# A hybrid encoder layer on one core: the recurrent chain's steps move off VectorE

## The chip, the cores and the metric

The kernel runs on one core of a Trainium2 chip. The time is the device time of one execution in microseconds. Of the engines, PE multiplies matrices, DVE and POOL work elementwise on vectors, ACT copies and evaluates functions, and SP starts most of the transfers. Each engine works through its own list of instructions in order.

## The reference

One layer over 1024 tokens of width 1024. A projection feeds two branches. The first is attention with a forgetting bias. The second is a recurrence with a state of 64x64 in each of 8 heads:

```python
def frame_step(state, inp):
    r_t, w_t, k_t, v_t, kk_t, a_t = inp
    sa = jnp.einsum('bhij,bhj->bhi', state, -kk_t)
    state = (state * w_t[:, :, None, :] + sa[..., None] * (kk_t * a_t)[:, :, None, :]
             + v_t[..., None] * k_t[:, :, None, :])
    return state, jnp.einsum('bhij,bhj->bhi', state, r_t)
```

The branches are gated, summed, projected and normalised. Then every token looks up experts: scores against keys, a top-k of 16 for each of 8 heads, and for each chosen expert a row of a table u and a row of a table v:

```python
h = jax.nn.gelu(jnp.einsum('thkd,td->thk', u_table[idx], xb), approximate=False)
return jnp.einsum('thk,thkd->td', gate * h, v_table[idx])
```

A second normalisation ends the layer.

## The kernel before

The tokens go in two halves of 512. For each half the kernel does the attention (`fox`), the recurrence (`rwkv_half`) and the merge with the first normalisation and the keys' scores (`merge_half`, `queries`). Behind both halves comes the dense stage (`dense_block`), which does three tiles of 128 tokens against all experts; the other five tiles are done with gathered rows.

The recurrence is done in chunks of 64 tokens, 8 chunks in a half, two heads (e = 0, 1) at a time. That makes four units in a half (`unit(ct)`). In a unit, PE makes the products of all chunks (tile pm, L915 to L916), and DVE masks them into M (L918): the first 64 columns with "not after", the last 64, called LT, with "before". Then a triangular system is inverted in six levels m = 0 to 5. In each, PE multiplies LT with Tm, DVE masks the product to the blocks of that level (x, L942), PE multiplies x with Vm, and DVE adds the results to Tm and Vm (L947, L952, L958). After the levels come W_, At (L993), Q (L999) and the eight steps of the state sigma, whose copies go to DVE and ACT by turns (L1010). `wait` lets in other work on PE between the steps: the projections of the next unit (`elem`), which end on DVE and ACT, and of the gates.

The order on PE is that of the code. On DVE, ACT and POOL a scheduler sets it when the kernel is built. Beside all this runs background work from the second half on, of two kinds: top-k of the scores on DVE (`topk`, from L1290), and expert rows gathered by POOL (L1389) into five buffers g, each multiplied with the token and summed on DVE (L1394, an instruction on 128x1024 and a short one that reads the sum). It is let in by `mm`: each matmul adds its reckoned time to a credit, and background steps are taken from the list while there is credit:

```python
us = max(n, 256) / 2400.0 if r.dtype == F32R else max(4 * n, 256) / 2400.0
g.V.tick(us)
if not g.V.busy:
    g.B.tick(us)
```

POOL also makes most of the low parts of the split weights (L295, wl) and a few steps of `elem` (L863, L864, L868, L883).

Of the kernel before, what the change touches and what calls it, by code (L numbers as in the profile page):

```python
# [83 lines left out]
def _tables():  # L84
# [11 lines left out]
    for m in (1, 2, 4, 8, 16, 32):  # L96
        lev.append(((s[:, None] // m) % 2 == 1) & (c64[None] // m == s[:, None] // m - 1))
# [624 lines left out]
def rwkv_half(g, hf, X, kt):  # L722
# [12 lines left out]
    with ExitStack() as fx:  # L735
# [164 lines left out]
        def unit(ct):  # L900
# [3 lines left out]
            def wait(us):  # L904
                F.fill(WAIT * us)

            items = [(e, c) for c in range(NC) for e in range(2)]
            M = cp.tile([128, 2, NC, 128], F32, name="M", bufs=1)
            BK = cp.tile([128, 2, NC, 64], F32, name="BK", bufs=1)
            AV = cp.tile([128, 3, NC, 64], F32, name="AV", bufs=1)  # L910
            for u in range(0, NC, 4):
# [5 lines left out]
                for e in range(2):  # L917
                    dve.tensor_mul(M[:, e, us, :], pm[:, e], tb("m1")[:, None, :].to_broadcast([128, 4, 128]))  # L918
# [11 lines left out]
            def LT(e, c):  # L930
                return M[rows[e], e, c, 64:128]

# [3 lines left out]
            Tm, Vm = None, None  # L936
            for m in range(6):
                px = psS.tile([128, NC, 64], F32, name="s")
                for e, c in items:
                    mm(g, px[rows[e], c, :], LT(e, c), i64[rows[e]] if Tm is None else Tm[rows[e], c, :], True, True)  # L940
                x = cp.tile([128, NC, 64], F32, name="x")
                dve.tensor_mul(x, px, lev[:, m:m + 1, :].to_broadcast([128, NC, 64]))  # L942
                wait(WT[2])
                if m < 5:
                    Tn = cp.tile([128, NC, 64], F32, name="Tm")
                    if Tm is None:
                        dve.tensor_add(Tn, x, i64b)  # L947
                    else:
                        pt = psS.tile([128, NC, 64], F32, name="s")
                        for e, c in items:  # L950
                            mm(g, pt[rows[e], c, :], Vm[rows[e], c, :], x[rows[e], c, :], True, True)
                        dve.tensor_add(Tn, pt, Tm)  # L952
                    Tm = Tn
                pv = psS.tile([128, NC, 64], F32, name="s")
                for e, c in items:
                    mm(g, pv[rows[e], c, :], x[rows[e], c, :], i64[rows[e]] if Vm is None else Vm[rows[e], c, :], True, True)
                Vn = cp.tile([128, NC, 64], F32, name="V")
                dve.tensor_add(Vn, pv, i64b if Vm is None else Vm)  # L958
                Vm = Vn
                wait(WT[3])  # L960
                if m == 1:

                    px = psS.tile([128, NC, 64], F32, name="s")
                    for e, c in items:
                        o = rows[1 - e]
                        mm(g, px[rows[e], c, :], M[o, e, c, 64:128], AV[o, e, c, :], True, True)
                    act.copy(AV[:, 2], px)
            wait(WT[4])
            W_ = cp.tile([128, NC, 64], F32, name="x")
# [13 lines left out]
            pa = psS.tile([128, NC, 64], F32, name="s")  # L983
            for e, c in items:
                r = rows[e]
                mm(g, pa[r, c, :], W_[r, c, :], BK[r, e, c, :], True, True)
            At = cp.tile([128, NC, 64], F32, name="Tm")
            if SM & 16:
                pool.tensor_mul(At, i64b, E.dgc[:, :, None].to_broadcast([128, NC, 64]))
                dve.tensor_add(At, At, pa)  # L990
# [3 lines left out]
            pq = psS.tile([128, NC, 64], F32, name="s")  # L994
            for e, c in items:
                r = rows[e]
                mm(g, pq[r, c, :], W_[r, c, :], M[r, e, c, 0:64], True, True)
            Q = cp.tile([128, NC, 64], F32, name="x")
            dve.tensor_add(Q, pq, arv[:, :, 0, :])  # L999
# [848 lines left out]
```

## Time and profile before

| | us |
|---|---|
| median of 3 runs | 3691.41 (3689.55 to 3696.35) |
| the profiled execution | 3689.26 |
| its span, first to last instruction | 3687.5 |
| PE busy in the span | 3232.5 (88%) |
| DVE busy | 2366.5 (64%) |
| POOL busy | 2243.2 (61%) |
| ACT busy | 1241.6 (34%) |

The shares are averages over stages of different kinds. The recurrence of the first half lies at about 180 to 480 us, that of the second half at about 1140 to 1555 us (four units of 103 to 105 us), the merge and the scores of the second half up to about 1870 us, and the dense stage from there on. A row of waits says which engine stood idle until which instruction of another had ended.

### The profile page before, as it was taken

To read this page: it belongs to the slowest core of one execution; us is meant where nothing else is said; L and a number is where in the kernel's file an instruction comes from. 1 tells how busy PE (TensorE), PEld (TensorE's weight loads), DVE (VectorE), ACT (ScalarE), POOL (GpSimd) and SP (SyncE) were. 2 spreads that over 40 slices of the span, in tenths; PEclk is the share of its full clock that TensorE was granted. 3 is DMA by queue.
4 is the path that set the end of the run, shared out by engine and by line. 5 is a ranking of instruction groups with operands and counts; after the bars stand their busy time and mean duration, and the time that the engine had idled before them with its cause. 6 is when DMAs were issued, how large, how long until landed. Compare 5 with 4: busy or idle time off the path is not lost. (4 is left out here: it accounts for less than half of the span.)

```text
span 3687.5 us, 55563 instructions
## 1 busy us (share of the span) xinstructions
PE 3232.5 (88%) x20656; PEld 2334.0 (63%) x20656; DVE 2366.5 (64%) x5125; ACT 1241.6 (34%) x2530; POOL 2243.2 (61%) x1752
## 2 busy tenths in 40 slices
PE   7899998989987877667868867899998999999998
PEld 5577777875565656546733322587776777777666
DVE  3235423558889998899669955477665767675324
ACT  3443222333443221222234433333333333333333
POOL 2031115326566556677846566688887888886773
PEclk9999999998888777889989989899999999999999
DMA  4121124548877777877869999899999999999994
GB/s 144 52 92 45 45 96 137 189 140 283 262 262 263 243 233 247 295 259 258 309 245 397 395 343 371 337 364 361 385 383 331 392 398 396 394 396 355 403 394 164
DMA packets 338127, 1019.61 MB, mean 277 GB/s; under 512 B 46272, under 2 KB 84928, under 8 KB 336064
## 3 DMA queue, kind: packets, MB, share of 16 engines
q0 software_dynamic: 184320, 671.17, 49.0%
q1 hardware_dynamic: 141424, 324.11, 24.7%
q10 hardware_dynamic: 12112, 20.78, 1.5%
q8 instruction: 162, 2.65, 0.3%
q14 instruction: 109, 0.89, 0.1%
HBM read 960.81 MB, written 55.12 MB: 276 GB/s over the span
## 5 line engine op out<-in xcount | busy, mean ns | idle before, releaser
L1389 POOL DMA_INDIRECT g<-u,eidx x640 | 789.0, 1233 | 397.1 <-DVE hh L1394 114.5
L1394 DVE CUSTOM_DVE_ANT_0 g<-g,ext 128x1024 f32<-128x1024 f32 x640 | 862.5, 1356 | 165.2 <-DMA g<-u,eidx 164.1
L295 POOL TENSOR_TENSOR wl<-wraw,wh 128x1024 fp32r<-128x1024 f32 x131 | 323.7, 2471 | 503.4 <-ACT wh L294 475.6
L1689 POOL DMA_INDIRECT vr<-v,ve x428 | 458.6, 1072 | 193.0 <-issue 99.9
L277 PE MATMUL pg<-vr,win 128*32 128x512 f32 x1712 | 322.4, 633 | 81.9 <-DMA vr<-v,ve 81.1
L277 PE MATMUL b<-xh,uh 128*128 128x384 f32 x1024 | 352.3, 344 | 22.1 <-DVE C L1574 22.0
L277 PE MATMUL b<-xh,ul 128*128 128x384 f32 x1024 | 348.9, 341 | 1.3 <-POOL ul L295 1.1
L277 PE MATMUL b<-xl,uh 128*128 128x384 f32 x1024 | 348.8, 341 | 0.0
L294 ACT CAST wh<-wraw 128x1024 fp32r<-128x1024 f32 x150 | 157.2, 1048 | 505.1 <-PE pj L277 280.2
L277 PE MATMUL v<-vl,ch 128*128 128x512 f32 x768 | 305.9, 398 | 11.2 <-POOL vl L295 11.1
L277 PE MATMUL pj<-xh,wh 128*128 128x512 f32 x624 | 289.9, 465 | 21.1 <-ACT xh L294 7.9
L277 PE MATMUL v<-vh,ch 128*128 128x512 f32 x768 | 303.3, 395 | 0.0
L277 PE MATMUL v<-vh,cl 128*128 128x512 f32 x768 | 301.4, 392 | 0.0
L1689 POOL DMA_INDIRECT C<-v,ve x212 | 225.6, 1064 | 84.8 <-issue 54.4
L294 ACT CAST uh<-uraw 128x512 fp32r<-128x512 f32 x256 | 158.2, 620 | 350.2 <-PE b L277 322.3
L277 PE MATMUL pj<-xh,wl 128*128 128x512 f32 x624 | 262.2, 420 | 4.3 <-POOL wl L295 2.5
L277 PE MATMUL pj<-xl,wh 128*128 128x512 f32 x624 | 263.1, 422 | 2.2 <-DVE xl L295 2.2
L294 ACT CAST vh<-vraw 128x512 fp32r<-128x512 f32 x256 | 157.7, 620 | 217.7 <-PE v L277 182.9
L277 PEld LDWEIGHTS b<-xh,uh 128*128 128x128 f32 x1024 | 194.1, 190 | 55.7 <-DVE C L1574 26.0
L295 POOL TENSOR_TENSOR ul<-uraw,uh 128x512 fp32r<-128x512 f32 x128 | 168.4, 1316 | 88.3 <-ACT uh L294 86.5
L295 DVE TENSOR_TENSOR vl<-vraw,vh 128x512 fp32r<-128x512 f32 x128 | 130.0, 1016 | 143.0 <-ACT vh L294 136.0
L277 PEld LDWEIGHTS b<-xl,uh 128*128 128x128 f32 x1024 | 194.2, 190 | 14.4 <-issue 10.1
(353 smaller groups left out, 6577.5 us busy)
## 6 DMA issues: line engine op xcount, KB each, us to landing
wraw<-w SPq DMA_DIRECT2D x150, 512.0 KB, 3.4
uraw<-ut SPq DMA_DIRECT2D x128, 512.0 KB, 6.6
vraw<-vt SPq DMA_DIRECT2D x128, 512.0 KB, 7.7
cd<-S SPq DMA_DIRECT2D x12, 1344.0 KB, 10.1
C<-cd SPq DMA_DIRECT2D x63, 256.0 KB, 9.2
g<-u,eidx POOLq DMA_INDIRECT x640
gtd<-tmp ACTq DMA_DIRECT2D x32, 256.0 KB, 4.3
g<-gtd SPq DMA_DIRECT2D x32, 256.0 KB, 3.7
```

Source lines behind the costliest of these rows:

```text
L277: g.pe.matmul(o, l, r, start=start, stop=stop_)
L294: g.act.copy(hi, src)
L295: (lo_eng or g.dve).tensor_sub(lo, src, hi.bitcast(F32))
L1389: pool.indirect_dma_start(out=gg, out_offset=None, in_=A["u"], in_offset=bass.IndirectOffsetOnAxis(ap=idx[:, s_:s_ + 1], axis=0))
L1394: dve.tensor_tensor_reduce(out=gg, in0=gg, in1=xt, scale=1.0, scalar=0.0, op0=OP.mult, op1=OP.add, accum_out=hh[:, k:k + 1])
L1689: g.pool.indirect_dma_start(out=place, out_offset=None, in_=g.A["v"], in_offset=bass.IndirectOffsetOnAxis(ap=self.meta[i][1][:, t:t + 1], ...
```

## The change

The tables of the levels' masks are turned, so that a mask is laid on LT itself and not on the product. ACT copies LT out of PSUM; POOL multiplies it with the mask of each level into L (three buffers), and adds L of level 0 and the identity into Vm. PE then multiplies with the masked L, and ACT copies the product to x. AK is the part of M that was used across the heads; M keeps the first 64 columns. This holds in both halves. In the second half (hf = 1) the sums go by PE as well: a multiplication of the old value with the identity is put into the same PSUM tile first, the products are added to it, and ACT copies the result. There M and AK are copied unmasked by ACT and masked in place by POOL, the diagonal of At is laid by POOL (dg), and all copies of sigma are ACT's. In the first half the sums stay on DVE. Behind `unit` the lines of the changed kernel are 51 higher than before.

```diff
@@ -94,7 +94,8 @@
     parts["m1"] = np.concatenate([s[:, None] <= c64[None], s[:, None] < c64[None]], 1)
     lev = []
     for m in (1, 2, 4, 8, 16, 32):
-        lev.append(((s[:, None] // m) % 2 == 1) & (c64[None] // m == s[:, None] // m - 1))
+
+        lev.append(((c64[None] // m) % 2 == 1) & (s[:, None] // m == c64[None] // m - 1))
     parts["lev"] = np.concatenate(lev, 1)
     parts["i64"] = s[:, None] == c64[None]
     rst = np.ones((128, 512))
@@ -905,9 +906,13 @@
                 F.fill(WAIT * us)
 
             items = [(e, c) for c in range(NC) for e in range(2)]
-            M = cp.tile([128, 2, NC, 128], F32, name="M", bufs=1)
+            M = cp.tile([128, 2, NC, 64], F32, name="M", bufs=1)
             BK = cp.tile([128, 2, NC, 64], F32, name="BK", bufs=1)
             AV = cp.tile([128, 3, NC, 64], F32, name="AV", bufs=1)
+
+            LT = cp.tile([128, NC, 64], F32, name="LT", bufs=1)
+            AK = cp.tile([128, NC, 64], F32, name="AK", bufs=1)
+            m1 = tb("m1").rearrange("p (a t) -> p a t", a=2)
             for u in range(0, NC, 4):
                 us = slice(u, u + 4)
                 pm = psM.tile([128, 2, 4, 128], F32, name="pm")
@@ -915,7 +920,17 @@
                     for e in range(2):
                         mm(g, pm[:, e, c, :], fl(bk[rows[e], u + c, e:e + 2, :]), fl(arv[rows[e], u + c, 0:2, :]), True, True)
                 for e in range(2):
-                    dve.tensor_mul(M[:, e, us, :], pm[:, e], tb("m1")[:, None, :].to_broadcast([128, 4, 128]))
+                    act.copy(LT[rows[e], us, :], pm[rows[e], e, :, 64:128])
+                for e in range(2):
+                    o = rows[1 - e]
+                    if hf:
+                        act.copy(AK[o, us, :], pm[o, e, :, 64:128])
+                    else:
+                        dve.tensor_mul(AK[o, us, :], pm[o, e, :, 64:128], m1[o, 1:2, :].to_broadcast([64, 4, 64]))
+                if hf:
+                    act.copy(M[:, :, us, :], pm[:, :, :, 0:64])
+                else:
+                    dve.tensor_mul(M[:, :, us, :], pm[:, :, :, 0:64], m1[:, 0:1, None, :].to_broadcast([128, 2, 4, 64]))
                 wait(WT[0])
                 pt = psM.tile([128, 2, 8, 64], F32, name="pm")
                 for c in range(4):
@@ -927,46 +942,76 @@
                 act.copy(AV[:, 0:2, us, :], pt[:, :, 4:8, :])
                 wait(WT[1])
 
-            def LT(e, c):
-                return M[rows[e], e, c, 64:128]
 
             lev = tb("lev").rearrange("p (m t) -> p m t", m=6)
             i64 = tb("i64")
             i64b = i64[:, None, :].to_broadcast([128, NC, 64])
-            Tm, Vm = None, None
+            L = []
             for m in range(6):
+                L.append(cp.tile([128, NC, 64], F32, name="L", bufs=3))
+                pool.tensor_mul(L[m], LT, lev[:, m:m + 1, :].to_broadcast([128, NC, 64]))
+                if m == 0:
+
+                    Vm = cp.tile([128, NC, 64], F32, name="V", bufs=1)
+                    pool.tensor_add(Vm, L[0], i64b)
+                if hf and m == 1:
+                    pool.tensor_mul(AK, AK, m1[:, 1:2, :].to_broadcast([128, NC, 64]))
+            if hf:
+                dg = cp.tile([128, NC, 64], F32, name="L", bufs=3)
+                pool.tensor_mul(dg, i64b, E.dgc[:, :, None].to_broadcast([128, NC, 64]))
+                for e in range(2):
+                    pool.tensor_mul(M[:, e], M[:, e], m1[:, 0:1, :].to_broadcast([128, NC, 64]))
+            def grown(t=None):
+
+                pt = psS.tile([128, NC, 64], F32, name="s")
+                if hf:
+                    mm(g, pt, ident, i64b if t is None else t, True, False)
+                return pt
+
+            def summed(pt, t=None):
+
+                o = cp.tile([128, NC, 64], F32, name="Tm", bufs=1) if t is None else t
+                if hf:
+                    act.copy(o, pt)
+                else:
+                    dve.tensor_add(o, pt, i64b if t is None else t)
+                return o
+
+            def last(c):
+                return not hf or c == NC - 1
+
+            pt = grown()
+            for e, c in items:
+                mm(g, pt[rows[e], c, :], L[0][rows[e], c, :], i64[rows[e]], not hf, last(c))
+            Tm = summed(pt)
+            wait(WT[3])
+            for m in range(1, 6):
                 px = psS.tile([128, NC, 64], F32, name="s")
                 for e, c in items:
-                    mm(g, px[rows[e], c, :], LT(e, c), i64[rows[e]] if Tm is None else Tm[rows[e], c, :], True, True)
-                x = cp.tile([128, NC, 64], F32, name="x")
-                dve.tensor_mul(x, px, lev[:, m:m + 1, :].to_broadcast([128, NC, 64]))
+                    mm(g, px[rows[e], c, :], L[m][rows[e], c, :], Tm[rows[e], c, :], True, True)
+                x = cp.tile([128, NC, 64], F32, name="x", bufs=1)
+                act.copy(x, px)
+                if m < 5:
+                    pt = grown(Tm)
                 wait(WT[2])
                 if m < 5:
-                    Tn = cp.tile([128, NC, 64], F32, name="Tm")
-                    if Tm is None:
-                        dve.tensor_add(Tn, x, i64b)
-                    else:
-                        pt = psS.tile([128, NC, 64], F32, name="s")
-                        for e, c in items:
-                            mm(g, pt[rows[e], c, :], Vm[rows[e], c, :], x[rows[e], c, :], True, True)
-                        dve.tensor_add(Tn, pt, Tm)
-                    Tm = Tn
-                pv = psS.tile([128, NC, 64], F32, name="s")
+                    for e, c in items:
+                        mm(g, pt[rows[e], c, :], Vm[rows[e], c, :], x[rows[e], c, :], not hf, last(c))
+                    summed(pt, Tm)
+                pv = grown(Vm)
                 for e, c in items:
-                    mm(g, pv[rows[e], c, :], x[rows[e], c, :], i64[rows[e]] if Vm is None else Vm[rows[e], c, :], True, True)
-                Vn = cp.tile([128, NC, 64], F32, name="V")
-                dve.tensor_add(Vn, pv, i64b if Vm is None else Vm)
-                Vm = Vn
+                    mm(g, pv[rows[e], c, :], x[rows[e], c, :], Vm[rows[e], c, :], not hf, last(c))
+                summed(pv, Vm)
                 wait(WT[3])
                 if m == 1:
 
                     px = psS.tile([128, NC, 64], F32, name="s")
                     for e, c in items:
                         o = rows[1 - e]
-                        mm(g, px[rows[e], c, :], M[o, e, c, 64:128], AV[o, e, c, :], True, True)
+                        mm(g, px[rows[e], c, :], AK[o, c, :], AV[o, e, c, :], True, True)
                     act.copy(AV[:, 2], px)
             wait(WT[4])
-            W_ = cp.tile([128, NC, 64], F32, name="x")
+            W_ = cp.tile([128, NC, 64], F32, name="x", bufs=1)
             for u in range(0, NC, 8):
                 n8 = min(8, NC - u)
                 us = slice(u, u + n8)
@@ -981,22 +1026,28 @@
                     (dve.tensor_copy if e and not SM & 32 else act.copy)(AV[r, e, us, :], pw[r, :, 64:128])
             wait(WT[5])
             pa = psS.tile([128, NC, 64], F32, name="s")
+            At = cp.tile([128, NC, 64], F32, name="Tm", bufs=1)
+            if hf:
+                mm(g, pa, ident, dg, True, False)
             for e, c in items:
                 r = rows[e]
-                mm(g, pa[r, c, :], W_[r, c, :], BK[r, e, c, :], True, True)
-            At = cp.tile([128, NC, 64], F32, name="Tm")
-            if SM & 16:
-                pool.tensor_mul(At, i64b, E.dgc[:, :, None].to_broadcast([128, NC, 64]))
-                dve.tensor_add(At, At, pa)
+                mm(g, pa[r, c, :], W_[r, c, :], BK[r, e, c, :], not hf, last(c))
+            if hf:
+                act.copy(At, pa)
             else:
                 for c in range(NC):
                     dve.scalar_tensor_tensor(At[:, c, :], i64, E.dgc[:, c:c + 1], pa[:, c, :], op0=OP.mult, op1=OP.add)
             pq = psS.tile([128, NC, 64], F32, name="s")
+            if hf:
+                mm(g, pq, ident, arv[:, :, 0, :], True, False)
             for e, c in items:
                 r = rows[e]
-                mm(g, pq[r, c, :], W_[r, c, :], M[r, e, c, 0:64], True, True)
-            Q = cp.tile([128, NC, 64], F32, name="x")
-            dve.tensor_add(Q, pq, arv[:, :, 0, :])
+                mm(g, pq[r, c, :], W_[r, c, :], M[r, e, c, :], not hf, last(c))
+            Q = cp.tile([128, NC, 64], F32, name="x", bufs=1)
+            if hf:
+                act.copy(Q, pq)
+            else:
+                dve.tensor_add(Q, pq, arv[:, :, 0, :])
             wait(WT[6])
             py = psS.tile([128, NC, 64], F32, name="s")
             for c in range(NC):
@@ -1007,9 +1058,9 @@
                     mm(g, pss[r, :], BK[:, e, c, :], AV[:, e, c, :], True, False)
                 for r in rows:
                     mm(g, pss[r, :], At[r, c, :], g.sigma[r, ct, par, :], False, True)
-                (act.copy if c % 2 or SM & 64 else dve.tensor_copy)(g.sigma[:, ct, 1 - par, :], pss)
+                (act.copy if c % 2 or hf else dve.tensor_copy)(g.sigma[:, ct, 1 - par, :], pss)
                 for e, r in enumerate(rows):
-                    mm(g, py[r, c, :], AV[:, e, c, :], M[:, e, c, 0:64], True, False)
+                    mm(g, py[r, c, :], AV[:, e, c, :], M[:, e, c, :], True, False)
                 for r in rows:
                     mm(g, py[r, c, :], g.sigma[r, ct, par, :], Q[r, c, :], False, True)
                 wait(WT[7])
```

On DVE in the third unit of the second half, just behind the projection of r, before (x, Tm and V are the chain's, s and ij the top-k's, g and hh the dot products'):

```order
L942 TENSOR_TENSOR x<-s,tab 128x512
L1351 TENSOR_TENSOR s<-s 128x4x128
L947 TENSOR_TENSOR Tm<-x,tab 128x512
L1351 TENSOR_TENSOR s<-s 128x4x64
L1394 ISA g,hh<-g,ext 128x1024
L1394 ISA hh 128x1
L1351 TENSOR_TENSOR s<-s 128x4x32
L958 TENSOR_TENSOR V<-s,tab 128x512
```

and in the same place now:

```order
L758 SCALAR_TENSOR_TENSOR rt<-prev,vec,tmp 128x1
L1343 MATCH_REPLACE tmp<-tv,s 128x128
L1348 MAX_INDEX ti<-tv,s 128x8
L1445 ISA g,hh<-g,ext 128x1024
L1445 ISA hh 128x1
L1345 MAX tv<-tmp 128x8
L1341 MAX tv<-s 128x8
```

The chain's steps are gone, and top-k and dot products stand close together.

On POOL at the end of the third unit and in the fourth, before (wl is a weight's low part, g a gather of 128 rows):

```order
L295 TENSOR_TENSOR wl<-wraw,wh 128x1024
L1389 DMA g<-u,eidx 128x1024 x15
L295 TENSOR_TENSOR wl<-wraw,wh 128x1024
L1389 DMA g<-u,eidx 128x1024 x2
L295 TENSOR_TENSOR wl<-wraw,wh 128x1024
L1389 DMA g<-u,eidx 128x1024 x23
```

and now (L and V are the chain's, M and AK the copies that are masked in place):

```order
L296 TENSOR_TENSOR wl<-wraw,wh 128x1024
L952 TENSOR_TENSOR L<-LT,tab 128x512 x2
L956 TENSOR_TENSOR V<-L,tab 128x512
L958 TENSOR_TENSOR AK<-AK,tab 128x512
L952 TENSOR_TENSOR L<-LT,tab 128x512
L963 TENSOR_TENSOR M<-M,tab 128x512 x2
L952 TENSOR_TENSOR L<-LT,tab 128x512
L1440 DMA g<-u,eidx 128x1024 x2
L952 TENSOR_TENSOR L<-LT,tab 128x512
L1440 DMA g<-u,eidx 128x1024 x4
L952 TENSOR_TENSOR L<-LT,tab 128x512
L1440 DMA g<-u,eidx 128x1024 x5
```

Eight steps on 128x512 stand in a row at the unit's head, and two more among the gathers.

On ACT in the third unit, at the middle of the levels, before (all of it is `elem` of the next unit):

```order
L861 COPY arv<-vt 128x8x64
L848 ACT_TABLE_LOAD
L848 ACTIVATE E_11594<-B 128x512
L846 ACTIVATE sw<-sw 128x512
L850 ACTIVATE B<-B 128x512
L871 ACTIVATE ag<-ag,oka,vec 128x512
```

and now:

```order
L849 ACT_TABLE_LOAD
L849 ACTIVATE E_11662<-B 128x512
L975 COPY Tm<-s 128x512
L975 COPY V<-s 128x512
L847 ACTIVATE sw<-sw 128x512
L851 ACTIVATE B<-B 128x512
L993 COPY x<-s 128x512
L975 COPY Tm<-s 128x512
L975 COPY V<-s 128x512
L872 ACTIVATE ag<-ag,oka,vec 128x512
```

The copies of the chain stand behind steps of `elem`, which wait for DVE.

## Rows read from the trace of the kernel before

**Rows 1.** Stretches: length; busy us (count) of PE, PEld, DVE, ACT, POOL; clock; DMA, GB/s.

```profile
1140.00:1555.00 415.00, 315.77 (x3778) 239.48 (x3777) 372.56 (x877) 85.32 (x135) 254.85 (x196) 0.79 0.75 256
...
1555.00:1760.00 205.00, 150.68 (x633) 114.26 (x632) 192.34 (x345) 53.30 (x72) 151.93 (x95) 0.90 0.76 260
```

**Rows 2.** PE's waits, 1140 to 1555 us: total us, times, longest.

```profile
PE s L277 <- DVE x L942: 38.1, 15, 10.1
PE s L277 <- DVE Tm L952: 17.8, 8, 5.5
PE s L277 <- DVE x L999: 15.7, 4, 6.4
```

**Rows 3.** DVE's waits, 1140 to 1555 us.

```profile
DVE g L1394 <- DMA g<-u,eidx: 20.6, 18, 2.9
DVE sigma L1010 <- PE s L277: 13.5, 8, 3.8
DVE M L918 <- PE pm L277: 4.1, 4, 1.6
...
DVE Tm L993 <- PE s L277: 1.2, 1, 1.2
```

**Rows 4.** DVE's timeline: start us, us, line, tiles, forms.

```profile
1306.54 1.22 DVE L1394 CUSTOM_DVE_ANT_0 g<-g,ext 128x1024 f32<-128x1024 f32 x1
1307.68 0.08 DVE L1394 DVE_READ_ACCUMULATOR2_ANT hh<- 128x1 f32 x1
...
1307.89 0.69 DVE L952 TENSOR_TENSOR Tm<-s,Tm 128x512 f32<-128x512 f32 x1
1308.49 0.28 DVE L1334 SCALAR_TENSOR_TENSOR ra<-pf,ra 128x128 bf16<-128x128 f32 x1
```

**Rows 5.** DVE's groups, 1140 to 1555 us: count, busy us, mean ns, idle before.

```profile
L1394 DVE CUSTOM_DVE_ANT_0 g<-g,ext 128x1024 f32<-128x1024 f32 x165 | 216.2, 1322 | 20.9 <-DMA g<-u,eidx 20.6
...
L1294 DVE MAX8 tv<-tmp 128x8 f32<-128x128 f32 x29 | 8.2, 283 | 0.0
...
L993 DVE SCALAR_TENSOR_TENSOR Tm<-tab,dgc,s 128x64 f32<-128x64 f32 x32 | 6.8, 276 | 1.2 <-PE s L277 1.2
L757 DVE SCALAR_TENSOR_TENSOR rt<-prev,vec,tmp 128x1 f32<-128x1 f32 x3 | 5.8, 1935 | 0.0
```

**Rows 6.** POOL's timeline at 1363 us.

```profile
1363.12 2.38 POOL L295 TENSOR_TENSOR wl<-wraw,wh 128x1024 fp32r<-128x1024 f32 x1
```

**Rows 7.** DVE's timeline at 1363 us.

```profile
1363.47 2.05 DVE L757 SCALAR_TENSOR_TENSOR rt<-prev,vec,tmp 128x1 f32<-128x1 f32 x1
```

**Rows 8.** POOL's groups, 1140 to 1555 us.

```profile
L1389 POOL DMA_INDIRECT g<-u,eidx x168 | 203.7, 1213 | 147.6 <-DVE hh L1394 56.5 <-issue 21.5 <-DVE ti L1299 18.5
L295 POOL TENSOR_TENSOR wl<-wraw,wh 128x1024 fp32r<-128x1024 f32 x15 | 37.7, 2510 | 10.1 <-ACT wh L294 9.9
L883 POOL TENSOR_TENSOR bkh<-bk,E 128x512 f32<-128x512 f32 x3 | 4.8, 1616 | 0.2
L863 POOL TENSOR_TENSOR arv<-rt,E 128x512 f32<-128x512 f32 x3 | 4.6, 1528 | 1.5 <-ACT E L848 1.4
```

**Rows 9.** ACT's groups, 1140 to 1555 us.

```profile
L967 ACT COPY AV<-s 128x512 f32<-128x512 f32 x4 | 2.3, 577 | 0.0
...
L848 ACT ACTIVATE E<-B 128x512 f32<-128x512 f32 x3 | 1.9, 631 | 18.2 <-DVE B L842 18.2
...
L758 ACT COPY prev<-pj 128x1 f32<-128x1 f32 x6 | 1.0, 159 | 16.5 <-DVE rt L757 8.3 <-DVE vt L757 8.1
```

**Rows 10.** PE's group of the bonus multiplication, 1140 to 1555 us.

```profile
L277 PE MATMUL s<-ag,tab 128*128 128x512 f32 x8 | 7.3, 1016 | 0.0
```

**Rows 11.** PE's waits, 1555 to 1760 us.

```profile
PE o L277 <- POOL wl L295: 11.8, 9, 2.5
...
PE b L277 <- DVE t L1335: 6.4, 1, 6.4
...
PE a L277 <- DVE kt L1072: 0.8, 1, 0.8
```

## The prediction

> **What bounds the kernel now.** I read the stretches of time first, then who waits for whom, then the groups of one engine. In the recurrent part of the second half (1140 to 1555 us) DVE is busy 372.6 of 415 us and PE 315.8 us at a granted clock of 0.79 [rows 1]. The reader is to see that the fullest engine there is DVE, and that PE's idle time is almost all DVE's making: PE waits 38.1 us for the masked x, 17.8 us for Tm and 15.7 us for the sum Q [rows 2]. DVE is full because background work (the expert dot products of L1394 and the top-k of L1290 and following) stands in its queue between the steps of the chain. Its own idle time is 20.6 us for gathered rows and 18.8 us for PE, on steps of the chain [rows 3]. After that, in 1555 to 1760 us, DVE is still busy 192 of 205 us [rows 1]. So from 1140 to 1760 us DVE sets the pace, and the question is what the change does to DVE's queue, not only what it does to the chain.
>
> **What leaves DVE.** Per unit 22 steps of 128x512 (4 for M, 6 for x, 5 for Tm, 6 for V, 1 for Q), 8 small ones for At and 4 copies of sigma. Back to back a 128x512 step takes 0.60 us (1307.89 to 1308.49) [rows 4]: 4 units x 22 x 0.60 = 53 us. The 32 steps of At are 6.8 us busy [rows 5], some 5 us of wall time, the 16 copies about 2 us: 60 us in all. DVE's waits for PE go too, since these steps are gone: 19 us [rows 3].
>
> **What comes to DVE.** Background steps are let in by the time that matmuls are reckoned at. The second half gets 12 multiplications with the identity in each unit, each 128x512, so more background is let in earlier. Counted in the lists of instructions, between the first bonus step (L896) and the group norm (L1052), there are 178 dot products where there were 163, and 325 top-k instructions where there were 212. A dot starts 1.14 us after the one before (1306.54 to 1307.68) [rows 4]: 15 x 1.14 = 17 us. A top-k instruction is 0.28 us [rows 5], with overlap some 0.26: 113 x 0.26 = 29 us. The whole up to the dense stage is the same in both, 384 dots and 744 top-k instructions, so these 46 us are taken off what follows.
>
> **What POOL's masks do to DVE.** 11 POOL multiplications or additions of 128x512 per unit are new, 44 in all. The nearest rows are 1.53 and 1.62 us for such a step with two inputs [rows 8]; with DVE not in the way I take 1.3 us, 57 us in all. They are not free for DVE: while POOL ran a split from 1363.12 for 2.38 us [rows 6], DVE's L757, one element per partition, took 2.05 us and ended with it [rows 7]; the same line's mean on rt is 1.94 us [rows 5]. Bounds: 0, if masks fell only beside steps that don't mind; 57 us, if each stopped DVE for its whole length. Between them lies what this stretch shows: the 165 dots average 1.322 us against 1.22 us undisturbed [rows 4, 5], 17 us, and L757 on rt another 5 us (5.8 us busy for three steps of one element) [rows 5], beside 47 us of two-input work on POOL [rows 8], so 0.47 us lost per us at least. I take 0.6: 34 us.
>
> The Trainium skill speaks against this change here ("SBUF — State Buffer", section "Who interferes with whom"): a DVE instruction with two SBUF inputs and a GpSimd instruction that reads SBUF take one shared port pair by turns, and the later is held for the earlier one's whole length. The trace agrees at 1363 us [rows 6, 7]; if every DVE step met it, the loss would be the 57 us above, and the sum 23 us worse; without the rule it would be 34 us better.
>
> **What POOL's masks do to the gathers.** The gathers of expert rows go by the same POOL queue. Eight mask steps now stand in a row before the next gather, and L4, L5 and the diagonal each wait for PE to release a buffer with gathers behind them. Eight steps at 1.3 to 1.6 us are 10 to 13 us; the five row buffers hold DVE's dots for 5 x 1.14 us plus the top-k between them, some 8 to 9 us. So DVE may stand dry for 2 to 4 us in a unit: 8 us over four. POOL has room (254.9 us busy of 415) [rows 1]: with 57 us of masks and 15 more gathers of 1.21 us [rows 8] it comes to 330 us.
>
> **ACT and PE.** ACT takes 19 copies of 128x512 more per unit at about 0.58 us [rows 9], and it is busy only 85 of 415 us [rows 1], so nothing by throughput. But ACT also holds steps that wait for DVE, and a copy of the chain queued behind them waits as well: 18.2 us before E<-B and 16.5 us before prev [rows 9]. As DVE sets the pace anyway, I count that at nothing of its own; if DVE didn't, it would keep up to 35 us of PE's present waits. On PE the 48 identity multiplications cost 1.8 us each at the low clock (8 records, 7.3 us, of 4 multiplications) [rows 10] and about 1.0 at the high one: 48 to 86 us, less a group of sixteen 64x64 multiplications per unit. PE comes to 360 to 400 us of 415. They stand where PE waited (99 us in all, of which the three rows of [rows 2] are 72), so they cost nothing unless DVE's queue gets short.
>
> **Sum for the recurrent part:** -60 - 19 + 17 + 29 + 34 + 8 = +9 us. The chain is freed, and DVE's queue still sets the time.
>
> **After it.** From 1555 us on DVE has 46 us less and POOL 15 gathers less. In 1555 to 1760 us PE waits 28 us for DVE (ten rows, from 6.4 to 0.8 us) and 16 us for POOL's weight splits (11.8 us in the largest) [rows 11]. I take two thirds of these 44 us, 30 us; bounds 10 and 44.
>
> **First half.** No background is on DVE there. Level 0 now waits for a POOL mask (1.5 us), and each unit loses one step of 0.6 us and one group of multiplications: between -4 and +6 us for four units, taken as 0.
>
> **Total:** +9 - 30 + 0 = -21 us. The profiled execution took 3689.3 us, so 3668 us; the median of the runs shown lies 2 us above it, so I write 3670 us.
>
> **Rivals.**
> *The pace passes to PE (large gain).* For it: PE's 99 us of waits were all but 1 us for DVE, and ACT and POOL are far from full. If masks cost DVE nothing (34 us less) and rows are always there (8 us less), the recurrent part falls by 33 us and the merge by 30 to 44: 3614 to 3628 us. Against it: rows 6 and 7, and DVE's list, no shorter than before.
> *No change.* The background moved out of the merge stage was filling slack there: PE then waits for weight splits, x and loads instead, and only some 10 us are won, which the +9 us eat: 3690 us. For it: POOL's splits are the largest wait there [rows 11]. Against it: DVE at 192 of 205 us.
> *POOL's queue starves DVE (slower).* The place is the head of each unit: eight masks in a row, each taking turns with a dot, 1.3 + 1.14 us, make 19.5 us without a gather against the 8 to 9 us that five rows last: 11 us dry per unit, 44 us instead of 8. It decides once the masks' stretch exceeds what the row buffers hold. That is 36 us more: 3706 us.
> That the change doesn't do what it says I exclude: the lists show no step of the chain on DVE in the second half.
>
> **How the numbers follow.** Forecast, a gain of 8 to 60 us: 0.50. Large gain: 0.13. No change: 0.13. Slower: 0.24. Two executions of this kernel differ by about 0.2%, 7 us, so that is the bound of "same": faster 0.63, same 0.13, slower 0.24. The range goes from the large gain's end to past the starving case, which with more loss to the port than 34 us would lie higher: 3615 to 3712 us. The forecast's own range is 3630 to 3684 us.
>
> **What would show it.** In the changed profile the recurrent part of the second half should last 400 to 440 us with DVE still 90% busy; PE's waits should stand on ACT copies and POOL masks, not on DVE's x, Tm or V, and be 40 to 60 us; L1394's mean should rise above 1.32 us, and DVE's wait for gathered rows above 20.6 us. The stretch from the group norm to the dense stage should be 20 to 40 us shorter. The dense stage should keep its length. I am wrong if the recurrent part gets shorter by over 30 us (the masks cost DVE little), if the dots stay at 1.32 us or less, or if the merge stage gains nothing.

## The result, and the profile after

The changed kernel took 3715.5 us (median of 7 runs, 3711.3 to 3721.1) against 3691.4 us before: ratio 1.0063, 95% interval 1.0046 to 1.0079. It is slower by 23 us; 3670 us was predicted. Each ratio below is to the kernel before on the same chip; the chips differ by 1.2% (before took 3733 us in the first group of runs, 3690 us in another), so traces of different chips are compared by stages, not by ends. Where ratios of different groups are set against each other, it is assumed that a ratio is the same on every chip; no run tests that. The profiled execution took 3721.1 us, the slowest of the seven, so its trace is 32 us longer than the one before, not 23.

By markers in the trace the first half ends its units at 531.9 us (535.1 before). The second group norm starts at 1591 us instead of 1555, the last score copy at 1891 instead of 1863, and the dense stage keeps its length within 4 us. So the recurrent part lost 36 us, and what follows, up to the last score copy, won back 7. Columns as in [rows 1], of the changed kernel: the recurrent part, group norm to last layer norm, from there to the last score copy.

```profile
1140.00:1591.00 451.00, 328.78 (x3734) 225.13 (x3734) 390.23 (x909) 144.60 (x263) 341.04 (x254) 0.84 0.73 252
1591.00:1768.00 177.00, 127.91 (x460) 95.03 (x461) 133.34 (x178) 39.77 (x52) 146.21 (x92) 0.84 0.80 278
1768.00:1891.00 123.00, 113.26 (x574) 96.57 (x573) 46.25 (x65) 34.92 (x53) 56.17 (x33) 0.92 0.59 200
```

The same two later stretches of the kernel before, where DVE is much fuller (PE is 5.4 us less busy in the two together, at a granted clock of 0.90 instead of 0.84 in the first):

```profile
1555.00:1728.00 173.00, 124.59 (x492) 91.80 (x491) 163.30 (x297) 43.13 (x57) 132.45 (x82) 0.90 0.75 254
1728.00:1863.00 135.00, 111.13 (x545) 92.10 (x543) 82.04 (x122) 36.23 (x54) 88.89 (x57) 0.92 0.80 278
```

DVE is 390.2 us busy in the recurrent part, 17.7 more than in [rows 1], and idle for 60.8 us instead of 42.4. Who waits for whom there, after: PE (to set beside [rows 2]), then DVE (beside [rows 3]), then DVE in the last unit and its backlog (1476 to 1591 us) alone.

```profile
PE s L278 <- POOL L L952: 45.3, 4, 21.4
PE s L278 <- ACT Tm L975: 19.7, 4, 9.0
PE s L278 <- ACT sw L835: 13.9, 2, 10.4
PE pj L278 <- POOL wl L296: 12.6, 3, 9.4
```

```profile
DVE g L1445 <- DMA g<-u,eidx: 55.9, 47, 10.6
DVE vt L897 <- PE s L278: 1.6, 1, 1.6
```

```profile
DVE g L1445 <- DMA g<-u,eidx: 39.8, 28, 10.6
```

PE no longer waits for DVE's x, Tm or Q; it waits for POOL's masks and ACT's copies. DVE no longer waits for PE; it waits 35 us longer for gathered rows, most of it in the last unit: top-k work had been used up in the unit before (DVE 98% busy, 127.5 us for that unit instead of 105.1), only dots were left, and a dot needs 1.14 us [rows 4] but its gather on POOL 1.29, with 0.3 us between most gathers:

```profile
1502.92 1.92 POOL L1440 DMA_INDIRECT g<-u,eidx  x1 [0.30 <-issue]
1505.14 1.41 POOL L1440 DMA_INDIRECT g<-u,eidx  x1 [0.30 <-issue]
```

The third and the last unit with its backlog, after; DVE's work stands in the third:

```profile
1348.50:1476.00 127.50, 84.30 (x932) 57.50 (x932) 124.63 (x314) 39.80 (x70) 92.52 (x68) 0.79 0.71 239
1476.00:1591.00 115.00, 82.98 (x950) 58.03 (x950) 72.93 (x113) 30.28 (x59) 89.98 (x68) 0.86 0.80 283
```

The longest single wait for rows lies at the head of the last unit, from 1514 to 1525 us, and most of it passes while POOL does the rest of its row of eight masks (1509 to 1521 us). The last unit's own steps end at 1579 us, 102 us after the third's, as long as before; the other 12 us pass until DVE reaches L1103, which the group norm needs and which stands in DVE's list behind dots, some of them waiting for rows. DVE, then ACT:

```profile
1524.95 1.23 DVE L1445 CUSTOM_DVE_ANT_0 g<-g,ext 128x1024 f32<-128x1024 f32 x1 [10.61 <-DMA g<-u,eidx]
```

```profile
1591.68 0.63 ACT L1105 ACTIVATE E<-kt 128x512 f32<-128x512 f32 x1 [12.02 <-DVE kt L1103]
```

Groups of DVE and of POOL in the recurrent part (beside [rows 5] and [rows 8]):

```profile
L1445 DVE CUSTOM_DVE_ANT_0 g<-g,ext 128x1024 f32<-128x1024 f32 x178 | 252.4, 1425 | 56.5 <-DMA g<-u,eidx 55.9
...
L1403 DVE TENSOR_TENSOR ij<-s 128x64 f32<-128x64 bf16 x8 | 13.0, 1622 | 0.1
```

```profile
L1440 POOL DMA_INDIRECT g<-u,eidx x182 | 234.4, 1288 | 97.2 <-issue 32.2 <-DVE hh L1445 16.0 <-DVE tmp L1343 12.6
...
L952 POOL TENSOR_TENSOR L<-LT,tab 128x512 f32<-128x512 f32 x24 | 30.0, 1256 | 6.8 <-PE s L278 6.7
L963 POOL TENSOR_TENSOR M<-M,tab 128x512 f32<-128x512 f32 x8 | 9.6, 1216 | 0.0
```

The head of the third unit, DVE and then POOL (start, us):

```profile
1374.70 12.03 DVE L1445 CUSTOM_DVE_ANT_0 g<-g,ext 128x1024 f32<-128x1024 f32 x1
1386.66 0.08 DVE L1445 DVE_READ_ACCUMULATOR2_ANT hh<- 128x1 f32 x1
```

```profile
1374.94 2.35 POOL L296 TENSOR_TENSOR wl<-wraw,wh 128x1024 fp32r<-128x1024 f32 x1
1377.23 2.13 POOL L952 TENSOR_TENSOR L<-LT,tab 128x512 f32<-128x512 f32 x2
1379.33 1.08 POOL L956 TENSOR_TENSOR V<-L,tab 128x512 f32<-128x512 f32 x1
...
1384.57 1.08 POOL L952 TENSOR_TENSOR L<-LT,tab 128x512 f32<-128x512 f32 x1
1385.80 1.78 POOL L1440 DMA_INDIRECT g<-u,eidx  x1 [0.15 <-issue]
```

One dot, 1.22 us undisturbed, took 12.03 us: it started 0.24 us before POOL's weight split and ended at 1386.73, a dot's length after the last mask (1385.65). POOL's instructions followed each other without a gap, and DVE got no turn between them. The next gather starts only at 1385.80. The row of the second unit held a DVE step in the same way:

```profile
1262.83 11.44 DVE L1403 TENSOR_TENSOR ij<-s 128x64 f32<-128x64 bf16 x1
```

In the rows of the first and of the last unit DVE and POOL took turns instead; first unit, DVE and then POOL:

```profile
1162.27 1.38 DVE L1445 CUSTOM_DVE_ANT_0 g<-g,ext 128x1024 f32<-128x1024 f32 x1
1164.05 1.63 DVE L1445 CUSTOM_DVE_ANT_0 g<-g,ext 128x1024 f32<-128x1024 f32 x1
```

```profile
1162.53 2.07 POOL L956 TENSOR_TENSOR V<-L,tab 128x512 f32<-128x512 f32 x1
1164.56 2.07 POOL L958 TENSOR_TENSOR AK<-AK,tab 128x512 f32<-128x512 f32 x1
```

What decides between the two was not tested. In the recurrent parts traced here and below, every DVE instruction held for more than 4.5 us had started while POOL was issuing a gather with the row right behind it; the dots that took turns had started during a mask or a split. Behind the group norm that pattern breaks: in the run with DVE's masks a dot that started during a split was held for 8.84 us.

### The profile page after: what moved, and what is told of

Its sections match the earlier page's. It is cut to its first block, busy times and chain, and to the rows that moved or that the text cites. A ratio compares the mean times of both kernels' runs of the same rounds, so it can differ in the third digit from the quotient of the medians.

```text
span 3719.3 us, 55464 instructions
## 1 busy us (share of the span) xinstructions
PE 3257.8 (88%) x20496; PEld 2324.1 (62%) x20496; DVE 2295.8 (62%) x4969; ACT 1314.8 (35%) x2690; POOL 2359.4 (63%) x1824
## 5 line engine op out<-in xcount | busy, mean ns | idle before, releaser
L1440 POOL DMA_INDIRECT g<-u,eidx x640 | 808.6, 1263 | 328.7 <-issue 99.3
L1445 DVE CUSTOM_DVE_ANT_0 g<-g,ext 128x1024 f32<-128x1024 f32 x640 | 883.1, 1387 | 211.0 <-DMA g<-u,eidx 209.8
L278 PE MATMUL pj<-xh,wl 128*128 128x512 f32 x624 | 258.2, 414 | 16.8 <-POOL wl L296 15.1
```

The costliest lines, as they stand in the source:

```text
L278: g.pe.matmul(o, l, r, start=start, stop=stop_)
L1440: pool.indirect_dma_start(out=gg, out_offset=None, in_=A["u"], in_offset=bass.IndirectOffsetOnAxis(ap=idx[:, s_:s_ + 1], axis=0))
L1445: dve.tensor_tensor_reduce(out=gg, in0=gg, in1=xt, scale=1.0, scalar=0.0, op0=OP.mult, op1=OP.add, accum_out=hh[:, k:k + 1])
```

## The experiments

Each difference between two ratios below is uncertain by some 0.25%, 9 us, so those of 10 to 14 us are only just there.

**Which part costs.** Three runs take one or both suspects out of the changed kernel. The first keeps the identity multiplications from admitting background:

```
-                    mm(g, pt, ident, i64b if t is None else t, True, False)
+                    pe.matmul(pt, ident, i64b if t is None else t, start=True, stop=False)
(pa and pq alike)
```

> The changed kernel, but the 12 identity multiplications of a unit don't admit background work; POOL's masks stay. By the lists DVE then has 287 dots instead of 306 before the second group norm, and as many top-k instructions (731). Credit theory (the extra background admitted is what makes the recurrent part long): 19 dots x 1.14 = 22 us off the 1140 to 1591 us stretch, some 8 us of it given back in the merge: 3698 to 3704 us. Port theory (POOL's rows of masks hold DVE) and queue theory (masks and gathers stand behind each other on POOL): the waits stay, since DVE there is held or dry and not only loaded; the third unit stays above 115 us, and the time at 3708 to 3717 us.

Measured 0.9985 (0.9971 to 0.9999): 29 us under the changed kernel, more than any of the theories gave. DVE's wait for rows stays (57.8 us), as the port and queue theories said, but the group norm starts at 1568 us. The 29 us are 1.5 us for each of the 19 dots, more than DVE's 1.14 us and about what a gather takes of POOL with the pause behind it; that it is POOL's time is argued, not shown.

The second puts the masks on DVE:

```
-                pool.tensor_mul(L[m], LT, ...)
+                (dve if hf else pool).tensor_mul(L[m], LT, ...)
(V, AK, dg and M of the second half alike)
```

> The changed kernel, but the second half's masks (11 steps of 128x512 a unit) are DVE's instead of POOL's; the sums still go by TensorE and ACT, the identity multiplications still admit background work. Port and queue theory: DVE gets 44 steps x 0.60 = 26 us, but no step of it is held for a row of masks (dots back from 1.43 to 1.32 us, 19 us; L1403 back from 13.0 to about 2 us, 11 us), PE's 45 us of waits for L shrink, DVE's wait for rows falls from 52 to 25 us: net 25 to 35 us less than the changed kernel, 3680 to 3690 us. Credit theory: DVE only gets 26 us more, 3735 to 3742 us.

Measured 0.9960 (0.9941 to 0.9979): 38 us under the changed kernel, with 26 us more work for DVE by the prediction's 0.60 us (the steps' mean was 0.78 us, because two of them took 2.83 and 3.24 us; the median is 0.68 us, as for the steps before, and in a row they follow each other every 0.60 us). DVE's wait for rows falls to 16.8 us. The pure credit theory is out.

> Both edits together: masks on DVE, and no background for the identity multiplications (281 dots and 686 top-k instructions before the second group norm, before the change 291 and 614). If both theories hold, their gains add: 3665 to 3680 us, below the kernel before. If only the port or the queue counts, it equals the run with DVE's masks alone, within 7 us. If only the credit counts, it is 22 us below that run but above the kernel before.

Measured 0.9916 (0.9896 to 0.9936): 54 us under the changed kernel, most of the 29 and 38 us of the two alone, and 31 us faster than before. The recurrent part ends at 1524 us, and PE runs at a granted clock of 0.92 there:

```profile
1140.00:1524.00 384.00, 328.87 (x3743) 226.21 (x3741) 343.67 (x845) 140.10 (x259) 248.66 (x185) 0.92 0.77 261
```

The fourth has the changed first half and the second half of before (`(unit_b if hf else unit)(ct)`, with the masks' table of before loaded for it).

> The first half as changed (masks ahead of the multiplications, level 0's multiplications saved), the second half as in the kernel before. The first half of the changed kernel ends its four units 3 us earlier by its trace (531.9 against 535.1 us). If nothing later swallows that, 3688 us (ratio 0.999); if the second half's loss is all that the change does otherwise, the rest of the trace lies on that of before.

Measured 0.9986 (0.9967 to 1.0006): the first half is worth between a gain of 12 and a loss of 2 us; the loss lies in the second.

**What a mask on POOL costs.** To the run with DVE's masks and no credit, 9 POOL steps a unit are added that change nothing: a second multiplication in place, or a copy in place.

```
+                    pool.tensor_mul(L[m], L[m], lev[:, m:m + 1, :].to_broadcast([128, NC, 64]))
(or)
+                    pool.tensor_copy(L[m], L[m])
(AK and M alike)
```

> The run with DVE's masks and no credit (0.9916 of before), plus 9 POOL steps a unit that multiply each already masked tile by its mask once more, in place (two inputs from SBUF, same result): the chain waits for POOL again and the gathers stand behind these steps, as in the changed kernel. 36 steps x 1.2 us = 43 us of POOL. Port theory: DVE is held for whole rows of them, L1445's mean goes from 1.35 to over 1.40 us with single dots of 5 us and more, and the time rises by 25 to 40 us: ratio 0.998 to 1.002. Queue theory: it rises as well, by 15 to 30 us (0.9955 to 1.000), through DVE's wait for rows and PE's wait for L, without long dots.

> As the run with the second multiplication on POOL, but each of the 9 POOL steps copies its tile onto itself: one input from SBUF instead of two; the lists of all engines stand in the same order. Port theory: what holds DVE is POOL's second input, so L1445's mean stays at 1.35 us with no dot over 3 us, and the time lies at 0.991 to 0.995, 20 us or more under the run that multiplies. Queue theory: gathers and PE wait behind these steps all the same; the two runs lie within 8 us of each other, and both over 15 us above 0.9916.

Multiplying: 1.0022 (1.0004 to 1.0039), 39 us over the base for 50.0 us of POOL. Copying: 0.9971 (0.9954 to 0.9989), 20 us for 35.6 us of POOL. The dots' means are 1.47 and 1.43 us, the longest 9.27 and 5.98 us. Neither theory's form held: copies cost half, not nothing, and they hold DVE as well. In the run with copies, DVE and then POOL:

```profile
1454.76 5.98 DVE L1449 CUSTOM_DVE_ANT_0 g<-g,ext 128x1024 f32<-128x1024 f32 x1 [0.49 <-DMA g<-u,eidx]
```

```profile
1455.11 2.35 POOL L296 TENSOR_TENSOR wl<-wraw,wh 128x1024 fp32r<-128x1024 f32 x1
1457.39 1.16 POOL L954 COPY L<-L 128x512 f32<-128x512 f32 x2
1458.50 0.60 POOL L961 COPY AK<-AK 128x512 f32<-128x512 f32 x1
1459.06 0.60 POOL L954 COPY L<-L 128x512 f32<-128x512 f32 x1
1459.62 1.59 POOL L967 COPY M<-M 128x512 f32<-128x512 f32 x1
```

The split ended at 1457.46; the dot waited through four copies more and ended at 1460.74, 1.08 us after the fourth. Here the fifth copy gave way: it took 1.59 us instead of 0.60. PE's wait for POOL's L is the same in both (13.3 and 13.4 us), DVE's for rows nearly (33.7 and 32.5 us). The longer steps hold DVE and fill POOL's queue for longer, and PE's wait for ACT's Tm, which no theory named, is 33.0 instead of 19.6 us; how the 19 us between the runs divide, they do not show.

The next puts V, AK, dg and M on DVE and leaves the six level masks on POOL, without credit (the first run's edit, and the second's without its first line).

> The changed kernel without credit, with only the six level masks on POOL; V, AK, M and the diagonal's mask (5 steps a unit) on DVE. POOL's row at the head of a unit is then 3 steps instead of 8. Port theory (cost by the row's length): nearer to the run with all masks on DVE than to the one with all on POOL: 0.992 to 0.995, longest dot under 5 us. Queue theory (the level masks are what the chain waits for, and they still stand between gathers): PE's wait for L stays at 13 us or more, DVE's wait for rows above 45 us, 0.996 to 0.999.

Measured 0.9948 (0.9928 to 0.9967): 12 us over the run with all masks on DVE. The time lies in the port theory's range and below the queue theory's. PE's wait for L (13.9 us) is what the queue theory gave, DVE's wait for rows (32.1 us) is not, and a dot of 7.0 us breaks the port theory's 'under 5 us':

```profile
1442.55 7.01 DVE L1445 CUSTOM_DVE_ANT_0 g<-g,ext 128x1024 f32<-128x1024 f32 x1 [0.77 <-DMA g<-u,eidx]
```

The 24 masks cost 0.5 us each, all 44 (the first run, 25 us) 0.57 each. That looks like a price by number, but 12 us uncertain by 9 cannot tell it from one by the row's length.

The last two put the masks on DVE in the last unit only (`dve if ct == 3 else pool`), or in the first three (`ct < 3`), credit as in the changed kernel.

> The changed kernel with the masks on DVE in the last unit of the second half only (11 steps); the other three units as changed. Starvation theory (in the changed kernel 40 of DVE's 56 us of waiting for rows fall in the last unit, where top-k is used up and POOL's masks stand behind and between gathers): most of the 38 us that masks on DVE bring in all four units come from this one, 25 to 35 us: ratio 0.997 to 1.000. Uniform theory (each mask on POOL costs the same wherever it stands): a quarter, 10 us: 1.003 to 1.005.

> The complement: masks on DVE in the first three units, on POOL in the last. Starvation theory: the last unit still runs at POOL's pace, at most 12 us come back: 1.003 to 1.0065. Uniform theory: three quarters, 28 us: 0.998 to 1.000.

Last unit: 1.0025 (1.0006 to 1.0045), 14 us less, and DVE's wait for rows falls from 55.9 to 38.9 us. First three: 0.9978 (0.9959 to 0.9997), 31 us less, wait 33.5 us. The uniform theory is the nearer, and the starvation theory's last-unit price is out: the 40 us wait shows in the last unit, but taking the masks off either part lowers it. With the last unit's masks on DVE that unit lasts 95 us instead of 102 and the group norm follows it at once (at 1573 us, the unit's end at 1572); the third unit stays at 126 us. Where the loss shows is not where it is caused: without credit (the first run) the third unit lasts 90.5 us and the fourth 129, where the changed kernel has 127.5 and 102. That earlier masks push background ahead of the last unit would explain it, and is not shown by itself.

**Which sums are worth moving.** Variants of the run with DVE's masks and no credit: V and Q summed by DVE; M and AK masked from PSUM; all sums on DVE.

```
-                pv = grown(Vm)
+                pv = grown(Vm, True)        (V: no identity, sum by DVE; Q alike)
```

> The run with DVE's masks and no credit, with V's four additions and Q's on DVE again (as before the change) and their five identity multiplications and ACT copies left out. DVE gets 20 x 0.60 = 12 us, PE loses 20 x 1.0 to 1.2 = 20 to 24 us. In that run PE was busy 329 of 384 us and DVE 344. If PE is the nearer bound by now, 5 to 15 us less: 0.9875 to 0.990. If DVE still sets the pace, 10 to 20 us more through DVE's queue standing in the chain again: 0.994 to 0.997.

Measured 0.9921 (0.9894 to 0.9947), no difference: PE loses 18 us of work, and waits 44 us for V and Q on DVE instead.

```
-                if hf:
-                    act.copy(M[:, :, us, :], pm[:, :, :, 0:64])
-                else:
-                    dve.tensor_mul(M...
+                if True:
+                    dve.tensor_mul(M...      (AK alike; their masks in SBUF go)
```

> The run with DVE's masks and no credit, but M and AK are masked by DVE straight from PSUM (as in the changed kernel's first half) instead of copied by ACT and masked in SBUF. ACT loses 6 copies a unit, DVE keeps the same steps at 0.60 instead of 0.77 us. If ACT's queue is the next limit (PE waited 16.8 us for its copy of AV there): 0.986 to 0.990. If PE then waits for DVE to empty the PSUM buffer instead (8.6 us for M in the kernel before): 0.991 to 0.995.

Measured 0.9943 (0.9927 to 0.9958): about 10 us worse than the base, just beyond the uncertainty. PE waits for DVE to empty its PSUM buffer, 30.9 us:

```profile
PE pm L934 <- DVE M L929: 30.9, 7, 12.4
```

All sums on DVE (each `hf` branch of the sums and of the copies of M and AK off; the masks DVE's):

> All sums of the second half on DVE again (T, V, A, Q), no identity multiplications, so no credit either; the masks are DVE's, on the copies ahead of the multiplications, M and AK from PSUM; x goes by ACT. DVE has per unit 12 masks and 11 sums, about the 23 steps of before. If taking the sums off DVE's queue is what gains: PE waits for DVE's Tm and Q again (17.8 and 15.7 us before), ratio 0.998 to 1.002. If moving the mask out of the chain (x: 38.1 us of PE's waits before) is what gains: 0.990 to 0.995.

Measured 0.9999 (0.9985 to 1.0014). PE waits for Tm again:

```profile
PE s L278 <- DVE Tm L977: 53.0, 14, 9.6
```

This run also masks M and AK from PSUM (10 us in the run before it), and V and Q on DVE cost nothing above, so some 20 of its 31 us over the base are left for the T and A sums, by differences that are each uncertain by 9 us; no run moves those alone. With the mask alone out of the chain nothing is gained: PE waits for the next DVE step instead (x: 38.1 us in [rows 2]). The rate alone (`RATEP = (1, 0.95, 0.9)` in the kernel before) does nothing:

> The kernel before, with background admitted at 0.95 of the reckoned matmul time in the recurrent part: 284 dots before the second group norm instead of 291, about as many as in the run with DVE's masks and no credit (281). If that run's gain over before (0.9916) came from admitting less and not from the chain's new form, this one gains as much: 0.990 to 0.994. If the chain's form counts, only 8 us of DVE are moved to the merge: 0.997 to 1.000.

Measured 0.9999 (0.9984 to 1.0013).

**What the stretch after the group norm gives back.** Three runs of the kernel before with work left out: 40 or 15 of tile 2's dots with their gathers, or the end of tile 3's top-k.

```
-    for s_ in range(128 + lead):
+    ns = 88 if tile_ == 2 else 128          (113 for the 15)
+    for s_ in range(ns + lead):
```

> The kernel before, with the last 40 of tile 2's 128 expert dots left out (its rows are not fetched either; tile 2's output is incomplete). Up to the second group norm the lists are as before (291 dots); after it 53 dots stand instead of 93, 40 x 1.14 = 46 us less of DVE, the same relief that the changed kernel brought there. The prediction's step (two thirds of the relief come back as time): group norm to last score 278 us instead of 308, ratio 0.990 to 0.993. Slack theory (PE waits there for weight splits, x and loads as soon as DVE's queue is short, as the changed kernel's 300 us show): 295 to 302 us, ratio 0.997 to 0.999.

> The kernel before, with the last 15 of tile 2's expert dots left out (tile 2's output is incomplete): the relief in dots that the changed kernel brought after the group norm. Theory A (0.72 us a dot, from 29 us for 40): 11 us less, group norm to last score 297 us, ratio 0.9965 to 0.998. If the gain for 40 came only from the end of the list running out early (a threshold): 0 to 3 us, 0.999 to 1.000.

```
-    for h0 in range(0, 8, TKI):
+    for h0 in range(0, 0 if tile_ == 3 else 8, TKI):     (and the loops that make ra, rb and ij)
```

> The kernel before, with the end of tile 3's top-k left out (84 DVE instructions after the second group norm, some 28 us; tile 3's experts are wrong). The changed kernel had 117 top-k instructions and 15 dots less there and came 7 us earlier from group norm to last score; 40 dots less brought 29 us. Theory A (what counts there is a dot with its gathered row, which share POOL's queue with the weight splits; top-k fills DVE's idle time): group norm to last score 300 to 312 us, ratio 0.998 to 1.001. Theory B (any DVE work counts at two thirds, as predicted): 19 us less, 289 us, ratio 0.994 to 0.996.

Measured 0.9933 (0.9913 to 0.9953), 0.9964 (0.9945 to 0.9983) and 0.9990 (0.9969 to 1.0012). By the traces group norm to last score takes 279, 294 and 310 us against 308 (the profiled execution of the third run is the slowest of its twelve). The last layer norm to the last score, with 40 dots, 15 dots and 84 top-k instructions less:

```profile
1729.00:1838.00 109.00, 105.74 (x572) 91.28 (x571) 24.75 (x42) 36.59 (x55) 35.34 (x17) 0.99 0.44 154
```

```profile
1733.00:1856.00 123.00, 109.26 (x573) 92.33 (x571) 63.73 (x92) 36.48 (x55) 70.14 (x43) 0.97 0.71 244
```

```profile
1742.00:1877.00 135.00, 112.36 (x546) 93.63 (x544) 67.43 (x93) 34.74 (x52) 79.43 (x48) 0.91 0.68 238
```

The last two differ by 3.7 us of DVE's busy time and 12 us of length, of which 3 us are PE's longer busy time at the lower granted clock (0.91 against 0.97): the time goes with the dots and gathers rather than with DVE's work. In the first, PE waits 11.1 us for POOL's weight splits instead of 21.5 before.

## Why the prediction was wrong

By the traces 51 us lie between the forecast (-21) and the outcome (+36 - 7 - 3 and 4 in the dense stage). Two steps of the sum hold nearly all of it: the gathers with 27 us and what comes after the recurrent part with 23.

- **What leaves DVE, what comes to it, what POOL's masks do to it** (-60 + 17 + 29 + 34 = +20 us): DVE's busy time rose by 17.7 us. As a sum right; the dots' mean rose from 1.322 [rows 5] to 1.425 us, 18 us in all, and the one long L1403 adds 11. But the hold is not always by turns, as the prediction took it: in two of the four rows POOL kept DVE out through all of it (12.03 and 11.44 us). The Trainium skill ("SBUF — State Buffer", "Who interferes with whom") has a two-input DVE instruction contend with any GpSimd instruction that reads SBUF; the copies' run agrees (5.98 us), and the trace adds that POOL's next instruction can go first, several times in a row.
- **DVE's waits for PE** (-19): 18.8 us in [rows 3], 1.6 us after. Right.
- **What POOL's masks do to the gathers** (+8): this step failed. It measured +35.3 us (20.6 to 55.9). It reckoned four dry spells of 2 to 4 us at the heads of the units and let POOL's room (255 us busy before, 341 after) stand for the rest; in the last unit, where only dots were left, the gathers came more slowly than the dots could take them. With the measured terms DVE's busy time and waits add up to +17.7 - 17 + 35 = +36, as busy and idle time must. That the masks on POOL are behind it is shown by the run that puts them on DVE: rows are waited for 16.8 us there. The rival "POOL's queue starves DVE" had the size (44 us), and 3706 us lay nearest. Its place, the head of a unit, shows once, with 10.6 us in the last unit; the first three units had 16 us of such waits together, and the other 29 us of the last unit come in waits of 0.2 to 5.5 us between its gathers.
- **ACT and PE** (nothing): PE's waits moved to ACT's copies and POOL's masks, as said, but L and Tm alone make 65 us, where 40 to 60 were given for all of them. In the last unit POOL issued 18 gathers and a split before the first mask, and PE stood 21.4 us for it: masks behind gathers were not weighed. The recurrent part lasted 451 us, beyond the 400 to 440 that were given as its sign, with DVE 87% busy.
- **After it** (-30): this step failed too, with 7 us. The rule was sound for dots (40 less: 29 us; 15 less: 14 us); it failed in pricing the 113 top-k instructions like dots. They fill time that DVE has (84 less: no gain in the trace, at most 11 us by the interval), so of the 46 us of relief only the 13 to 15 dots matter. By the runs these should have brought 11 to 14 us; why it was 7 is open, PE's 5.4 us more of busy time at the lower clock being one candidate.
- **First half** (0, -4 to +6): -3 us by the trace. Right.

The identity multiplications' background was priced as DVE time (17 us for 15 dots) and cost more: the run without it, 19 dots less, starts the group norm 23 us earlier and is 29 us faster. Each dot brings a gather to POOL, which is the likely reason.

## What to carry to other kernels

Before a step is moved to an engine that also feeds another by its queue, price that queue: here masks on POOL cost 0.5 to 0.9 us each more than on DVE (24 of them 12 us, 44 of them 25 us, or 38 us with the extra background), although DVE was the fullest engine. Background work isn't one currency: find which of it holds the scarce resource (here a dot with its gather), and count that. The form that gained (0.9916) moved the sums to TensorE and ACT, kept the masks on DVE, and let no more background in.

## What the runs showed of the hardware

POOL instructions that follow each other without a gap can keep a DVE instruction with two SBUF inputs waiting through all of them: 12.03 us for a dot, 11.44 us for L1403's 128x64 step. They need not: in two of the four rows dots and masks alternated, with masks of 2.07 us. POOL copies with one input hold such a dot too (5.98 us, through a split and four copies). A 128x512 mask took DVE 0.68 us (median) with both operands in SBUF and with one in PSUM, 0.60 us apart in a row; on POOL it took 1.08 us in a row that held DVE, and a copy 0.60 us. A gather of 128 rows took POOL 0.93 us at the least and 1.29 us in the mean, with 0.3 us before the next.
